# When the quarter sums of a token operand are made: behind the fifth and the sixth tile's rows, or all behind the fifth's

## The chip, the cores and the metric

The kernel runs on one core of one Trainium2 chip. The metric is device time in microseconds (us), the median of several runs. TensorE (PE in the profile) multiplies matrices and PEld loads its weights; VectorE (DVE), ScalarE (ACT) and GpSimd (POOL) work element by element; SyncE (SP) issues DMAs. Each engine runs its own queue of instructions in order and waits on semaphores of the others.

## The reference, cut to what matters

Two layers of a bidirectional encoder trunk on 1024 tokens and 16 meta tokens of width 1024: a mixer (gated DeltaNet and a short convolution) and then a SwiGLU feed-forward of inner width 2816, each with an RMSNorm before it and a residual after it. Only the feed-forward's first matrix product matters here:

```python
def swiglu(h, w_gate_up, w_down):
    gate, up = jnp.split(h @ w_gate_up.astype(h.dtype), 2, axis=-1)
    return (jax.nn.silu(gate) * up) @ w_down.astype(h.dtype)
...
h = h + swiglu(rmsnorm(h, norm2_w[l]), w_gate_up[l], w_down[l])
```

Everything is float32. The kernel splits each operand in two parts (a rounded `hi`, copied by ACT, and a rest `lo = x - hi`, made by DVE) and makes each product with three matmuls.

## The kernel before, in words

A layer goes through input projection, the DeltaNet scan, output projection, gate-and-up product, down product. The stage of this change is gate and up: a loop over 22 tiles `f` of 128 inner channels, numbered from 0, so that the "fifth tile" is `f == 4` (`NE = 4`) and the "sixth" is `f == 5`.

For each tile the gate and the up weights are two 128-column strips of 1024 rows. The kernel takes gate and up, the two halves of the 1024 inputs and the two halves of the tokens as a 2 by 2 matrix product, and makes it with seven products in place of eight (a Strassen-Winograd scheme): `p1` to `p7`, with weight sums and differences (`S1` at L1464, `S2` at L1465, `S3` at L1486, `S4` at L1485) and token operands that are the same for all tiles, `T["B11"]`, `T["B21"]`, `T["T1"]` to `T["T4"]` and `T["B22"]`, made before the loop. Each weight operand is split by `w_op` (L1104 on ACT, L1105 on DVE) into one of seven slots, which come free as PE has read them. The weights come by DMA (L1456 to L1459) into small rings of buffers.

Tiles 6 to 17 are taken in pairs, even and odd. Their `p3`, the product of `S4` and `T["B22"]`, is not made alone: `block()` makes it for the two tiles together, again as a 2 by 2 product in seven smaller ones of a quarter of the tokens each (`bp`, matmuls at L1530 to L1532). For this it needs
- weights: `keep`, which is `S4` of the even tile (L1485), the odd tile's counterpart `s1t` (L1473), and `sm`, four sums and differences of the two (L1476 to L1479), all split by `w_op`;
- tokens: the four quarters of `T["B22"]` themselves and four sums of these quarters, split and kept in `TB[0]` to `TB[3]`. These are the quarter sums of this change. They are made once in a layer, by `block_operands`, and read by every pair.

The sums are made in scratch tiles `c4k("t")`, each cut in two halves `va` and `vb`. The tag "c" of `c4k` has two buffers in the whole kernel, and `keep` and `sm` come from the same two. Tokens are 1040 columns in layer 0 and 1024 in layer 1, so a sum of two half-quarters works on 128 x 520 or 128 x 512 elements.

`row_end` closes a tile: it scales gate and up (L1438, L1439), applies silu (L1440), multiplies (L1441, `row_done`), and stores the row (L1445). `row_before` is the `row_done` of the tile before. `after(a, b)` makes instruction `a` wait for `b`.

The order on each engine is set when the kernel is built, by a planner that runs through the program with a model of times. Each instruction's rank is its place in the program unless the code gives it another; of the instructions that can start by the model, the one of the first rank goes next, and a tile gets a buffer of its ring when the model has one free. At run time each engine keeps that order.

The function `block_operands(i)` is called twice in a layer: with 0 after tile 4's `row_end` and with 2 after tile 5's. Each call makes two sums; its first instruction waits for the row just ended, and the second call's second sum needs the first call's second sum (`less`). The first pair of tiles that reads the result is 6 and 7.

## Time and profile before

| | us |
|---|---|
| median of 3 runs | 2468.67 |
| lowest and highest run | 2467.69, 2473.94 |
| the profiled execution | 2466.03 |
| its span, first to last instruction | 2464.3 |
| PE busy in the span | 2438.2 (99%) |
| DVE busy | 1834.9 (74%) |
| ACT busy | 1081.9 (44%) |

All times inside the profile count from the start of the span. The tiles of interest lie at 688 to 730 us in layer 0 and at 1908 to 1948 us in layer 1. A busy PE is not PE at its full pace: matmuls overlap, and their length also grows when the granted clock falls, so the number of matmuls in a stretch is read beside the busy time.

In a row of the timeline stand the start, the busy time, the engine, the line, the operation, the tile written and those read (buffer numbers left out), the shape, and in brackets how long the engine had been idle and what released it. Tiles named `a`, `b`, `P` are slices of large buffers that many operands share, so the line tells more than the name. In a row of a window stand the stretch, its length, the busy time and count of PE, PEld, DVE, ACT and POOL, the granted TensorE clock as a share, the DMA share and GB/s.

### The profile page before, as it was taken

How to read it: one execution, taken by the hardware profiler on the slowest of the kernel's cores; microseconds unless marked ns; L12 is line 12 of the kernel's file. 1: busy time of each engine (PE TensorE's matmuls, PEld its weight loads, DVE VectorE, ACT ScalarE, POOL GpSimd, SP SyncE). 2: the span in 40 equal slices, each digit the busy share in tenths (PEclk: the TensorE clock that was granted, in tenths of full speed). 3: DMA queues.
4: the chain of work that ended last, by engine and by line, in shares of the span. 5: the costliest groups of instructions: out<-in, count | busy, mean ns of one | idle time of the engine just before them, and what ended most of it. 6: DMA issues, size and time to landing. Idle time of an engine off the chain costs nothing. (4 is left out here: it accounts for less than half of the span.)

```text
span 2464.3 us, 45203 instructions
## 1 busy us (share of the span) xinstructions
PE 2438.2 (99%) x17602; PEld 2256.7 (92%) x17602; DVE 1834.9 (74%) x3436; ACT 1081.9 (44%) x2028; POOL 66.3 (3%) x157
## 2 busy tenths in 40 slices
PE   9999999999999999999999999999999999999998
PEld 8999999999999999999999988998978788888887
DVE  6888346769888887977657984457797888778775
ACT  6654434536333333444445543345453333334544
POOL 0120000000000000000001100000000000000002
PEclk9999999999999999999999999999999999999999
DMA  4445345534222224674224453445332222337641
GB/s 134 160 156 185 118 134 158 182 101 134 100 78 104 84 86 137 223 243 143 92 81 155 155 179 111 152 144 194 121 124 98 82 94 99 119 130 251 198 136 69
DMA packets 201322, 335.27 MB, mean 136 GB/s; under 512 B 23404, under 2 KB 88356, under 8 KB 201108
## 3 DMA queue, kind: packets, MB, share of 16 engines
q1 hardware_dynamic: 172996, 293.83, 36.0%
q10 hardware_dynamic: 25936, 34.19, 4.3%
q0 software_dynamic: 2176, 4.36, 0.6%
q8 instruction: 138, 2.26, 0.4%
q14 instruction: 76, 0.62, 0.1%
HBM read 250.31 MB, written 81.99 MB: 135 GB/s over the span
## 5 line engine op out<-in xcount | busy, mean ns | idle before, releaser
L168 PE MATMUL pacc<-a,whi 128*128 128x346 f32 (+1 forms) x800 | 260.1, 326 | 0.7 <-ACT whi L138 0.4
L170 PE MATMUL pacc<-a,wlo 128*128 128x346 f32 (+1 forms) x800 | 259.0, 325 | 0.1
L168 PE MATMUL pacc<-b,whi 128*128 128x346 f32 (+2 forms) x672 | 232.4, 347 | 0.0
L170 PE MATMUL pacc<-b,wlo 128*128 128x346 f32 (+2 forms) x672 | 231.5, 346 | 0.0
L169 PE MATMUL pacc<-a,whi 128*128 128x346 f32 (+1 forms) x681 | 221.8, 326 | 0.2 <-DVE a L189 0.2
L138 ACT ACTIVATE whi<-raw 128x512 fp32r<-128x512 f32 x166 | 104.4, 631 | 236.8 <-PE pacc L169 195.1
L169 PE MATMUL pacc<-b,whi 128*128 128x346 f32 (+2 forms) x580 | 200.1, 345 | 0.0
L139 DVE TENSOR_TENSOR wlo<-raw,whi 128x512 fp32r<-128x512 f32 x166 | 114.0, 688 | 53.5 <-ACT whi L138 52.8
L168 PEld LDWEIGHTS pacc<-a,whi 128*128 128x128 f32 x800 | 150.5, 188 | 3.0 <-issue 1.0
L170 PEld LDWEIGHTS pacc<-a,wlo 128*128 128x128 f32 x800 | 150.7, 189 | 1.4 <-issue 0.8
L170 PEld LDWEIGHTS pacc<-b,wlo 128*128 128x128 f32 x672 | 126.4, 188 | 10.2 <-issue 1.7
L168 PEld LDWEIGHTS pacc<-b,whi 128*128 128x128 f32 x672 | 126.4, 188 | 9.8 <-issue 0.8
L169 PEld LDWEIGHTS pacc<-a,whi 128*128 128x128 f32 x681 | 128.3, 188 | 4.1 <-issue 2.1
L169 PEld LDWEIGHTS pacc<-b,whi 128*128 128x128 f32 x580 | 109.2, 188 | 7.9 <-issue 1.0
L1104 ACT ACTIVATE whi<-rw 128x512 fp32r<-128x512 f32 (+1 forms) x82 | 49.8, 615 | 107.4 <-PE pacc L1125 36.1
L1104 ACT ACTIVATE b<-rw 128x512 fp32r<-128x512 f32 (+1 forms) x63 | 38.7, 620 | 102.3 <-PE pacc L1125 29.0
L331 DVE TENSOR_TENSOR b<-pacc,rstd 128x346 f32<-128x346 f32 (+1 forms) x63 | 32.3, 513 | 49.0 <-PE pacc L170 46.3
L1104 ACT ACTIVATE a<-rw 128x512 fp32r<-128x512 f32 (+1 forms) x63 | 38.5, 618 | 64.4 <-PE pacc L1125 17.2
L331 DVE TENSOR_TENSOR a<-pacc,rstd 128x346 f32<-128x346 f32 (+2 forms) x59 | 32.6, 553 | 42.5 <-PE pacc L170 41.9
L1105 DVE TENSOR_TENSOR wlo<-rw,whi 128x512 fp32r<-128x512 f32 (+1 forms) x82 | 54.1, 666 | 9.9 <-ACT whi L1104 9.4
L1368 ACT ACTIVATE P<-a 128x512 fp32r<-128x512 f32 x63 | 38.3, 625 | 25.4 <-PE pb L1684 19.7
L1368 ACT ACTIVATE P<-b 128x520 fp32r<-128x520 f32 x63 | 37.2, 628 | 27.1 <-PE pacc L1684 20.1
(1129 smaller groups left out, 8019.0 us busy)
## 6 DMA issues: line engine op xcount, KB each, us to landing
raw<-in_w_in SPq DMA_DIRECT2D x110, 256.0 KB
raw<-in_w_gu SPq DMA_DIRECT2D x104, 256.0 KB
rw<-in_w_gu SPq DMA_DIRECT2D x88, 256.0 KB
rw<-in_w_dn SPq DMA_DIRECT2D x90, 192.0 KB
rec<-vkd SPq DMA_DIRECT2D x61, 256.0 KB
raw<-in_w_out SPq DMA_DIRECT2D x48, 256.0 KB
b<-ad SPq DMA_DIRECT2D x45, 260.0 KB
a<-ad SPq DMA_DIRECT2D x45, 256.0 KB
```

The source lines that it names most:

```text
L138: whi_done[0] = hasten(wpr, lambda: act(out=hi, in_=raw[:, 0:kk, :], func=AF.Copy))
L139: whi_done[1] = hasten(wpr, lambda: tt(out=lo, in0=raw[:, 0:kk, :], in1=hi.bitcast(F32), op=ALU.subtract))
L168: mm(ps[:, :n], wh, xh[:, n0:n1], start=(i == 0), stop=False)
L169: mm(ps[:, :n], wh, xl[:, n0:n1], start=False, stop=False)
L170: last_mm[0] = mm(ps[:, :n], wl, xh[:, n0:n1], start=False, stop=(i == K - 1))
L331: tt(out=t[:, n0:n1], in0=ps, in1=rstd[:, n0:n1], op=ALU.mult)
L1104: hasten(wpr, lambda: act(out=hi, in_=src, func=AF.Copy))
L1105: hasten(wpr, lambda: tt(out=lo, in0=src, in1=hi.bitcast(F32), op=ALU.subtract))
L1368: act(out=hi, in_=r, func=AF.Copy)
```

## The change

All four sums of a layer are now issued after tile 5's `row_end`, in two calls, and wait only for tile 4's row (`gate[0]`). The first call (`late` False) makes sums 0, 1 and 3 in one scratch tile, sum 3 in place over sum 1; the second (`late` True) makes sum 2 in another. In each call the difference `cx - cy`, which waits for no row, now stands first. Each sum is split right after it is made (`put`).

```diff
-        TB, us, rows, less = [], [], [], [None]
+        TB, us, rows, gate = {}, [], [], []
...
-        def block_operands(i):
+        def block_operands(late):
...
-            x, cx, y, cy, p, q = (b22, c22, b12, c12, b21, c21) if i else (b12, c12, b11, c11, b22, c22)
             va, vb = (t.rearrange("p (k e) -> p k e", k=2) for t in halves(c4k("t"), 2 * E))
-            after(tt(out=va, in0=x, in1=y, op=ALU.subtract), row_before)
-            tt(out=vb, in0=cx, in1=cy, op=ALU.subtract)
-            tt(out=va, in0=va, in1=vb, op=ALU.add)
-            tt(out=vb, in0=p, in1=less[0] if i else va, op=ALU.subtract)
-            tt(out=vb, in0=vb, in1=q, op=ALU.add)
-            less[0] = vb
-            for r, v in zip(rows[i:i + 2], (va, vb)):
-                h, w = (t.rearrange("p (k e) -> p k e", k=2) for t in halves(r, 2 * E))
+            x, cx, y, cy = (b22, c22, b12, c12) if late else (b12, c12, b11, c11)
+
+            def put(n, v):
+                h, w = (t.rearrange("p (k e) -> p k e", k=2) for t in halves(rows[n], 2 * E))
                 act(out=h, in_=v, func=AF.Copy)
                 tt(out=w, in0=v, in1=h.bitcast(F32), op=ALU.subtract)
-                TB.append((h, w))
+                TB[n] = h, w
+
+            tt(out=vb, in0=cx, in1=cy, op=ALU.subtract)
+            after(tt(out=va, in0=x, in1=y, op=ALU.subtract), gate[0])
+            tt(out=va, in0=va, in1=vb, op=ALU.add)
+            put(2 if late else 0, va)
+            for n, p, q, less in () if late else ((1, b22, c22, va), (3, b21, c21, vb)):
+                tt(out=vb, in0=p, in1=less, op=ALU.subtract)
+                tt(out=vb, in0=vb, in1=q, op=ALU.add)
+                put(n, vb)
...
-            if f in (NE, NE + 1):
-                block_operands(2 * (f - NE))
+            if f == NE:
+                gate.append(row_before)
+            if f == NE + 1:
+                block_operands(False)
+                block_operands(True)
```

## The prediction

> **What bounds the kernel now.** I read the page's busy table first, then the busy time and granted clock in 10 us windows over the whole span, then, where TensorE lost time, the waits of PE, the chain that ended last and the order of instructions on DVE.

> ```profile
> PE 2438.2 (99%) x17602; PEld 2256.7 (92%) x17602; DVE 1834.9 (74%) x3436; ACT 1081.9 (44%) x2028; POOL 66.3 (3%) x157
> 700.00:720.00 20.00, 20.00 (x169) 20.00 (x168) 17.31 (x32) 7.26 (x16) 0.00 (x0) 1.00 0.26 90
> 720.75:729.22 8.47, 6.55 (x38) 5.88 (x37) 7.11 (x14) 2.67 (x6) 0.00 (x0) 0.80 0.09 32
> 1900.00:1920.00 20.00, 20.00 (x88) 16.22 (x87) 15.94 (x24) 7.00 (x11) 0.00 (x0) 1.00 0.24 92
> 1935.35:1948.13 12.78, 7.06 (x29) 5.68 (x27) 12.39 (x23) 5.12 (x10) 0.00 (x0) 0.73 0.18 62
> ```

> TensorE sets the time: 99% of the span. A change that moves work on DVE and ACT can only matter where PE stops. The window rows read: stretch, its length, then busy time (count) of PE, PEld, DVE, ACT and POOL, and the granted clock. Ahead of the final tail only two of the 10 us windows have a clock under 1.00, and both are the first product block of a layer (tiles 6 and 7). Layer 0: 38 matmuls took 8.47 us; at the pace beside it (20/169 = 0.118 us) they need 4.5, so 4.0 us are lost. Layer 1: between the edges stand 24 narrow matmuls of the block (0.118 us each, 2.8) and three wide ones (20/88 = 0.227, 0.7) in 12.78 us, so 9.3 are lost. Together 13.3 us, 0.54% of the span: that is the most this change can win. Of it 1.9 (8.47 - 6.55) and 5.7 (12.78 - 7.06) is standing still, the rest, 2.1 and 3.6, slower pace.

> PE's waits (line that waited, what it waited for, us in total, times, longest) and the chain in layer 1 say for whom it stood still:

> ```profile
> PE pf L1530 <- ACT b L1104: 3.2, 1, 3.2
> PE pf L1532 <- DVE b L1105: 1.8, 1, 1.8
> PE pacc L1532 <- DVE a L1105: 1.1, 1, 1.1
> PE pa L1530 <- DVE a L1509: 0.7, 1, 0.7
> ```
> ```profile
> 1936.39 0.68 DVE a L1431
> 1937.07 0.60 DVE t L1426
> 1937.67 0.60 DVE keep L1485
> ```

> Each wait of the block's lines (L1530 to L1532) occurs once in the run, so the later block tiles have none of this size. In layer 1 the chain runs through the very instructions the change moves: the sums (L1426, L1431), then `keep`, the weight difference of tile 6 (L1485); `sm` (L1476), which holds the block's other weights, comes after them. The order on DVE shows why these follow each other:

> ```profile
> 1907.18 1.23 DVE L1441 TENSOR_TENSOR b<-b,b3f 128x1024 f32<-128x1024 f32 x1
> 1910.72 0.69 DVE L1422 TENSOR_TENSOR t<-a 128x512 f32<-128x512 f32 x1
> 1920.28 0.68 DVE L1426 TENSOR_TENSOR t<-t,a 128x512 f32<-128x512 f32 x1
> 1921.48 0.69 DVE L1473 TENSOR_TENSOR rw<-raw,rw 128x512 f32<-128x512 f32 x1
> 1922.95 0.69 DVE L1431 TENSOR_TENSOR a<-t,a 128x512 fp32r<-128x512 f32 x1
> 1928.81 0.69 DVE L1582 TENSOR_TENSOR b<-pb,b 128x512 f32<-128x512 f32 x1 [5.17 <-PE pb L1126]
> 1931.28 1.22 DVE L1441 TENSOR_TENSOR b<-b,a3f 128x1024 f32<-128x1024 f32 x1
> 1933.35 0.68 DVE L1422 TENSOR_TENSOR t<-a 128x512 f32<-128x512 f32 x1
> 1937.59 0.69 DVE L1485 TENSOR_TENSOR keep<-raw,rw 128x512 f32<-128x512 f32 x1
> 1939.92 0.69 DVE L1431 TENSOR_TENSOR b<-t,b 128x512 fp32r<-128x512 f32 x1
> 1941.13 0.42 DVE L1476 TENSOR_TENSOR sm<-rw 128x256 f32<-128x256 f32 x1
> ```

> Row 5 (the second L1441) ends at 1932.5; only then may the second call begin (1933.35). Both calls' scratch, `keep` and `sm` share two buffers (tag "c" in the code). The first call's buffer is held for `less` until the second call reads it (L1425), so `keep` comes at 1937.59; the second call's is held until its last split (1939.92), and `sm` follows at 1941.13. PE had run out of other work at 1935.35.

> **The change part by part.**

> *Count.* Before: two calls with 5 sums and 2 splits on DVE each, 14 in a layer, and 4 copies on ACT. After: 10 and 4 on DVE, 3 and 1 on ACT. Nothing is added; no DMA, no matmul. Cost of the amount itself: zero.

> *The second call leaves row 5's end.* Six of its seven DVE instructions stood behind row 5 (its L1423 is ungated and ran earlier). At the 0.6 us by which successive ones start (1937.07 to 1937.67 in the chain) that is 3.6 us of DVE work in a layer that goes from behind row 5 to before it. What it frees is worth more than its length: `keep` and `sm` no longer wait for row 5. Gated on row 4, ending at 1907.18 + 1.23 = 1908.4, 12 DVE instructions remain to be done (14 less the two ungated first differences). At 0.6 us that is 7.2 us, so 1915.6 at best. At worst they go at the present first call's pace: seven from 1910.72 to 1923.64, 1.85 us each, 22.1 us, so 1932.8. I take 1921, nearer the best: tile 7's preparation, which now shares that stretch with them, ranks behind the sums in the new order, tile 5's own read-outs come only as PE delivers them, and DVE stands idle 5.17 us before 1928.81. From `keep`'s place to the first block split is 0.7 us on DVE and another on ACT; to `sm` it is 3.5 (1937.59 to 1941.13). `sm` also needs L1473, at 1921.48 now; if the 3.6 us push that to 1925, `sm` is ready around 1929, its splits around 1932, still before 1935.35. So layer 1's stall goes whole: 9.3.

> ```profile
> 698.93 0.69 DVE L1431 TENSOR_TENSOR b<-t,b 128x520 fp32r<-128x520 f32 x1
> 708.75 1.23 DVE L1441 TENSOR_TENSOR a<-a,b3f 128x1040 f32<-128x1040 f32 x1
> 715.19 0.68 DVE L1485 TENSOR_TENSOR keep<-raw,rw 128x512 f32<-128x512 f32 x1
> 722.14 0.69 DVE L1464 TENSOR_TENSOR rw<-rw,rw 128x512 f32<-128x512 f32 x1 [1.36 <-DMA rw<-in_w_gu]
> 722.75 0.69 DVE L1105 TENSOR_TENSOR a<-sm,a 128x512 fp32r<-128x512 f32 x1
> ```

> Layer 0 has the same order: row 5 to 710.0, `keep` at 715.19. The last thing late there is the split of `sm` (722.75), queued on DVE behind an addition of tile 8 that waited for its load. That load takes a buffer which tile 7's work frees, so it too starts sooner when `keep` and `sm` do. With the worst pace (first call 689.4 to 699.6, seven, so 12 take 17.5 us from 688) the sums end at 705.5 and `keep` comes some 9 us earlier than now, against a stall of 4. I take all 4.0; if the load did not move, the 4.0 stay.

> *What the added DVE load may cost in tile 5.*

> ```profile
> 688.00:710.00 22.00, 22.00 (x186) 22.00 (x185) 19.78 (x35) 7.54 (x14) 0.00 (x0) 1.00 0.24 78
> 1908.00:1932.00 24.00, 24.00 (x105) 19.50 (x104) 18.61 (x29) 6.67 (x11) 0.00 (x0) 1.00 0.15 55
> ```

> From row 4's to row 5's end DVE has 2.2 us free in layer 0 and 5.4 in layer 1. Adding 3.6 overfills layer 0 by 1.4 us; what spills is tile 7's preparation, which finds the 3.6 us vacated behind row 5. So it costs PE between 0 and 1.4; I take the middle, 0.7. In layer 1 it fits.

> *The in-place fourth sum.* It overwrites the second sum, so DVE must wait until ACT has copied it.

> ```profile
> 1922.22 0.62 ACT L1430 ACTIVATE a<-t 128x512 fp32r<-128x512 f32 x1
> 1931.40 0.42 ACT L1104 ACTIVATE b<-rw 128x256 fp32r<-128x256 f32 x1 [8.56 <-issue]
> ```

> The present second sum is done at 1920.96 and its copy at 1922.84: 1.9 us, in which DVE had other instructions. Between 0 (others stand there) and 8.56 us (ACT once stood that long at a weight copy; everything behind the sum on DVE, tile 5's read-outs included, would wait). Nearest is the 1.9, under the idle time of tile 5 in layer 1 and inside the 0.7 in layer 0: no further cost.

> *The slower pace.* After standing still in layer 0, PE started a matmul every 0.21 us (726.43 to 726.64) instead of every 0.12, until 729.03:

> ```profile
> 726.43 0.42 PE L1531 MATMUL pf<-b,a 128*128 128x260 f32 x1
> 726.64 0.42 PE L1532 MATMUL pf<-b,a 128*128 128x260 f32 x1
> ...
> 729.03 0.36 PE L1125 MATMUL pf<-P,whi 128*128 128x260 f32 x1
> ```

> It follows the stall in both layers and no other place, so I count it as part of the stall. [...]

> **Sum.** 9.3 + 4.0 - 0.7 = 12.6 us. The profiled execution took 2466.03 us, so 2453.4; it lies 2.6 under the median of the runs (2468.67), so the median comes to 2456.1.

> **The rivals.**

> (B) Layer 1 is freed only in part. At the worst pace above, `keep` comes at 1932.8, 4.8 us sooner than now; layer 1 then saves 4.8 of its 9.3, layer 0 its 4.0: 8.8 less, 2459.9. For it: DVE was full from 1910 to 1923. Against: the 5.17 us gap after that.

> (C) The change doesn't do what it says: the sums have the lowest rank among tile 5's work, and if the last split of the third sum is still put behind row 5, one of the two "c" buffers stays taken, `sm` stays late, and the time stays at 2468.7.

> ```profile
> L1423 DVE TENSOR_TENSOR t<-b x2: 692/692/693, 607.7 to 690.0; 128x520 f32<-128x520 f32 x2
> ```

> For it: of the two ungated differences of layer 0 the second stood at 690.0 only, among the gated ones. Against: the first ran at 607.7, 82 us ahead of them, so what nothing holds is moved early.

> (D) Slower: the in-place sum becomes the wait. If ACT stands for w us in front of the second sum's copy, DVE stands with it, 2w in two layers, plus the 1.4 overfill less 1.8 left in layer 1 (5.4 - 3.6), plus slow pace as now (2.1 + 3.6), against the 13.3 won: 2w - 8. It breaks even at w = 4 and is over 7.4 us slower from w = 7.7. With the 8.56 of the ACT row: +9.1, 2477.8. Against it: the copies of the sums waited 1.9 at most. [...]

> **How the numbers follow.** Forecast 0.52, B 0.16, C 0.18, D 0.14. 0.3% (7.4 us) is about what a measurement of this kernel tells from no change; the limits are 2461.3 and 2476.1. The forecast and three quarters of B are faster: 0.64. The rest of B and nearly all of C are the same: 0.20. D and a little of C are slower: 0.16. The range runs from 2453 (all 13.3 off the fastest run, 2467.69, and 1.4 for other gains) to 2470 (C); it leaves out D. The forecast's own range is 2453 to 2458.5, its upper end being the sum in which layer 0's slow pace stays.

> **What would show it.** Right: all the sums start between row 4's and row 5's end; `keep` before row 5's end in both layers; no PE wait over 0.5 us on L1530 or L1532; granted clock 1.00 through both places; DVE over 21 us busy in the 22 of layer 0's tile 5. Wrong: a wait of DVE on the ACT copy in front of the in-place sum of over 4 us, a wait of PE at L1122 to L1126 in tile 6 or 7 that is not there now, or sums behind row 5.

## The result, and the profile after

The changed kernel takes 2461.54 us (median of 6 runs, 2458.01 to 2462.64) against 2468.99 (6 runs, 2467.69 to 2473.94): a ratio of 0.9964, 95% interval 0.9951 to 0.9977, so 7.45 us less. A second series gave 2459.91 against 2467.89 (0.9970, 0.9958 to 0.9982), 7.98 less. The sign is the forecast one and the time lies in the range, but the forecast was 12.6 us less. The profiled execution of after took 2462.45 us with a span of 2460.7. One execution, of the kernel called the gate alone below, took 11524.8 us for a reason that no profile shows, and is left out of every number.

At the two places of the change the profile looks as forecast. Windows of after (stretch, length, busy time and count of PE, PEld, DVE, ACT, POOL, granted clock, DMA share, GB/s):

```profile
690.35:712.35 22.00, 22.00 (x186) 22.00 (x185) 21.47 (x41) 9.01 (x16) 0.00 (x0) 1.00 0.32 105
718.00:728.00 10.00, 10.00 (x86) 10.00 (x85) 8.68 (x17) 4.40 (x9) 0.00 (x0) 1.00 0.20 67
1910.96:1937.57 26.61, 26.61 (x119) 21.66 (x119) 24.16 (x40) 9.25 (x16) 0.00 (x0) 1.00 0.19 70
1935.00:1948.00 13.00, 11.99 (x66) 10.02 (x65) 13.00 (x23) 6.04 (x11) 0.00 (x0) 1.00 0.28 99
```

The clock is 1.00 through both blocks. In layer 0, 86 matmuls fit into 10 us in which before had 56:

```profile
718.00:728.00 10.00, 8.08 (x56) 7.41 (x55) 8.10 (x17) 3.57 (x7) 0.00 (x0) 0.89 0.17 54
```

The order on DVE in layer 1 (timeline of after; `keep` is now L1489, `sm` L1480, the row's product L1445):

```profile
1909.73 1.23 DVE L1445 TENSOR_TENSOR b<-b,b3f 128x1024 f32<-128x1024 f32 x1
1913.28 1.28 DVE L1430 TENSOR_TENSOR t<-a 128x512 f32<-128x512 f32 x2
1927.65 0.68 DVE L1489 TENSOR_TENSOR keep<-raw,rw 128x512 f32<-128x512 f32 x1
1929.63 0.69 DVE L1426 TENSOR_TENSOR b<-t,b 128x512 fp32r<-128x512 f32 x1 [0.70 <-ACT b L1425]
1932.68 0.41 DVE L1480 TENSOR_TENSOR sm<-rw 128x256 f32<-128x256 f32 x1
1936.35 1.22 DVE L1445 TENSOR_TENSOR b<-b,a3f 128x1024 f32<-128x1024 f32 x1
1937.49 0.42 DVE L1483 TENSOR_TENSOR sm<-keep,sm 128x256 f32<-128x256 f32 x1
1938.42 0.68 DVE L1105 TENSOR_TENSOR b<-sm,b 128x512 fp32r<-128x512 f32 x1
1940.23 0.68 DVE L1105 TENSOR_TENSOR wlo<-sm,whi 128x512 fp32r<-128x512 f32 x1
```

All the instructions of the sums that wait for row 4 (1913.28 to 1930.32) lie between row 4's and row 5's end, and `keep` comes before row 5's product. Of the four instructions of `sm` three come before it and the last (1937.49) behind it, and so do the two splits of `sm` (1938.42 and 1940.23); in layer 0 all of `sm` comes behind row 5 (715.54 for a row that ends at 715.15). What the prediction did not have stands elsewhere, in the waits of PE:

```profile
PE pa L1122 <- DVE a L1573: 2.2, 1, 2.2
PE pa L1122 <- ACT b L1104: 1.6, 1, 1.6
PE pf L1534 <- ACT sm L1542: 1.0, 1, 1.0
```

The wait at L1534, the first of the block's lines (L1530 before), lies in layer 1's block. The wait of 2.2 us is new and lies in layer 1's tiles 0 to 2, some 75 us ahead of the changed instructions of that layer. Before, the read-out of tile 0 (L1569) stood early on DVE; after, it (L1573) stands three instructions further back, and the first of the two read-outs has moved behind an addition that waits 1.88 us for weights from DMA, though PE's last matmul into `pb` had ended at 1827.79. Timeline of before, then of after:

```profile
1828.63 0.68 DVE L1566 TENSOR_TENSOR a<-pb,b 128x512 f32<-128x512 f32 x1
1830.55 0.69 DVE L1464 TENSOR_TENSOR rw<-rw,rw 128x512 f32<-128x512 f32 x1 [1.24 <-DMA rw<-in_w_gu]
1831.76 0.69 DVE L1569 TENSOR_TENSOR a<-pa,a 128x512 f32<-128x512 f32 x1
```

```profile
1830.71 0.69 DVE L1468 TENSOR_TENSOR rw<-rw,rw 128x512 f32<-128x512 f32 x1 [1.88 <-DMA rw<-in_w_gu]
1831.92 0.68 DVE L1570 TENSOR_TENSOR a<-pb,b 128x512 f32<-128x512 f32 x1
1834.33 0.68 DVE L1573 TENSOR_TENSOR a<-pa,a 128x512 f32<-128x512 f32 x1
```

To see where each kernel gains and loses, I take the start of the n-th matmul of its trace (all traces hold 17602) less that in before, and list how this difference grows in seven stretches, named by the times of before. Negative is a gain. One profiled execution stands behind each row. Mostly near the blocks (694 to about 1080 and 1920 to 2100 us) the order of the matmuls differs from kernel to kernel, so that the n-th is not always the same one.

| kernel | to 688 | 688-735 | 735-1810 | 1810-1840 | 1840-1908 | 1908-1960 | to the end |
|---|---|---|---|---|---|---|---|
| after | +2.4 | -4.2 | +1.6 | +2.7 | 0.0 | -7.7 | +1.6 |
| after, second series | +0.8 | -4.2 | +0.3 | +3.9 | 0.0 | -7.7 | +0.3 |
| gate alone | +0.3 | -4.2 | +0.4 | +2.5 | 0.0 | -8.5 | -0.3 |
| gate alone, second series | +7.1 | -4.2 | +0.7 | +3.9 | 0.0 | -8.5 | -0.7 |
| gate alone, layer 1 order | +1.1 | -4.2 | -0.6 | +0.2 | 0.0 | -8.4 | -0.2 |
| after, layer 1 order | +0.7 | -4.2 | +1.7 | +1.6 | 0.0 | -7.7 | +0.8 |
| after, fourth sum not in place | +2.7 | -4.2 | +0.7 | +4.0 | 0.0 | -8.7 | -0.2 |
| after, gate on row 5 | +0.9 | +3.2 | +0.9 | +2.4 | 0.0 | +2.7 | +0.9 |
| before, one scratch tile | +1.5 | -3.2 | +0.7 | -0.2 | 0.0 | -2.1 | +0.4 |
| gate alone, one scratch tile | +1.0 | -4.2 | +2.6 | -0.2 | 0.0 | -4.8 | -0.3 |
| after, `keep` behind row 5 | +0.8 | -4.1 | +0.5 | +2.9 | 0.0 | -5.8 | +0.7 |
| after, `keep` later still | +0.8 | -1.6 | +0.8 | +1.9 | 0.0 | -0.4 | +0.4 |

The first column has nothing of the change in it: two executions of the same kernel differ there by 6.8 us (gate alone), so a single execution tells little by its whole time. The two block columns repeat within 0.1. So the two blocks gave 11.9 us, and layer 1's start took 2.7 to 3.9 of it back. Taken on to 2060 us, where the order of these kernels is the same again, layer 1's block is still at -7.7 in both profiles of after, but at -9.0 and -9.1 in the two of the gate alone and at -9.2 with the fourth sum not in place.

### The profile page after: what moved, and what is told of

It is laid out like the page before. It is cut to its first block, busy times and chain, and to the rows that moved or that the text cites. A ratio compares the mean times of both kernels' runs of the same rounds, so it can differ in the third digit from the quotient of the medians.

```text
span 2460.7 us, 45205 instructions
## 1 busy us (share of the span) xinstructions
PE 2436.8 (99%) x17602; PEld 2255.1 (92%) x17602; DVE 1834.7 (75%) x3436; ACT 1082.1 (44%) x2028; POOL 66.4 (3%) x157
## 5 line engine op out<-in xcount | busy, mean ns | idle before, releaser
L1104 ACT ACTIVATE whi<-rw 128x512 fp32r<-128x512 f32 (+1 forms) x82 | 49.9, 616 | 107.2 <-PE pacc L1125 36.7
L1104 ACT ACTIVATE b<-rw 128x512 fp32r<-128x512 f32 (+1 forms) x63 | 38.8, 620 | 98.4 <-PE pacc L1125 32.3
L1104 ACT ACTIVATE a<-rw 128x512 fp32r<-128x512 f32 (+1 forms) x63 | 38.5, 618 | 68.3 <-PE pb L1125 17.5
L1105 DVE TENSOR_TENSOR wlo<-rw,whi 128x512 fp32r<-128x512 f32 (+1 forms) x82 | 54.1, 665 | 11.8 <-ACT whi L1104 11.1
```

Of the source, the lines that this page charges most:

```text
L1104: hasten(wpr, lambda: act(out=hi, in_=src, func=AF.Copy))
L1105: hasten(wpr, lambda: tt(out=lo, in0=src, in1=hi.bitcast(F32), op=ALU.subtract))
```

## The experiments

Theory 1: the gate does the work. What stalls the block is that `keep`, `sm` and their splits stand behind row 5 and the sums on DVE. Theory 2: PE waited for the sums themselves, or the new grouping and the in-place sum matter. Theory 3: the missing gain went at layer 1's start, by the order of instructions there. The ratios are to the kernel before in the same series, whose medians were 2469.35, 2468.44 and 2467.89 us.

**The gate alone.** Before, with only the second call's gate moved to row 4.

```diff
-            after(tt(out=va, in0=x, in1=y, op=ALU.subtract), row_before)
+            after(tt(out=va, in0=x, in1=y, op=ALU.subtract), gate[0])
...
+            if f == NE:
+                gate.append(row_before)
```

> The kernel before, with one edit: the second call's first sum waits for tile 4's row in place of tile 5's. The grouping of the sums, their scratch and the sum that isn't in place stay as before. Theory 1 (the late gate keeps both 'c' buffers taken, and keep and sm come late): the gate alone is the change; both stalls go, some 2461.5 us, within 2 of the changed kernel. Rival (the regrouping and the in-place sum matter too): less than half of the gain, over 2465.

Measured: 2458.66 us (5 runs), ratio 0.9958 (0.9946 to 0.9971). The gate alone carries the whole gain; it came out 2.9 us under the changed kernel, not within the 2 expected. Both blocks lose their stall, layer 1's by 8.5 (9.0 up to 2060 us).

**The changed kernel with the gate on row 5.** Same grouping and in-place sum; only the gate is late.

```diff
-            if f == NE:
-                gate.append(row_before)
             if f == NE + 1:
+                gate.append(row_before)
                 block_operands(False)
                 block_operands(True)
```

> The changed kernel, with one edit: all sums wait for tile 5's row. Theory 1: twelve instead of six DVE instructions of the sums now stand between row 5 and the last split, 0.6 us each, so keep and sm come up to 3.6 us later than in the kernel before: stalls as before or longer, 2469 to 2476. Rival (the regrouping is the gain, not the gate): 2461 to 2463.

Measured: 2477.22 us (5 runs), ratio 1.0033 (1.0020 to 1.0046): slower than before, and a little beyond the range expected. Both calls now stand behind row 5 and the stalls are longer than ever. PE's waits:

```profile
PE pf L1534 <- ACT b L1104: 6.1, 1, 6.1
PE pacc L1534 <- ACT a L1104: 2.8, 1, 2.8
```

The grouping of the calls, with its in-place sum, is no gain of its own; with the old gate it loses 8 us.

**The fourth sum not in place.** After, with the second and fourth sum divided over the calls as before.

```diff
-            for n, p, q, less in () if late else ((1, b22, c22, va), (3, b21, c21, vb)):
-                tt(out=vb, in0=p, in1=less, op=ALU.subtract)
-                tt(out=vb, in0=vb, in1=q, op=ALU.add)
-                put(n, vb)
+            n, p, q, less = (3, b21, c21, sums[0]) if late else (1, b22, c22, va)
+            tt(out=vb, in0=p, in1=less, op=ALU.subtract)
+            tt(out=vb, in0=vb, in1=q, op=ALU.add)
+            sums.append(vb)
+            put(n, vb)
```

> After, with the second and the fourth sum grouped as before (the fourth is made in the second call's own scratch from the kept second one, nothing is overwritten). If the about 3 us by which the gate alone beat the changed kernel come from the in-place sum, directly or through the DVE order that it brings with it (in this kernel the read-outs of tile 0 in layer 1 stand as early as with the gate alone): about 2458.7 us, no wait over 1 us at pa L1122. If they come from the order of the calls (difference cx - cy first, both calls after tile 5): about 2461.5.

Measured: 2458.95 us (0.9962, 0.9949 to 0.9974). The expectation was wrong on one point: the wait at L1122 stayed (2.1 us), since the read-outs stand just as far back as in the changed kernel. Its layer 1 block is 1.0 better (-8.7 for -7.7, and -9.2 for -7.7 up to 2060 us), and it has no wait at the block's L1534. By the medians it seemed 2.6 better than after, as the gate alone seemed 2.9 better; so both kernels were run again.

**After and the gate alone, once more, on one chip.**

> The changed kernel once more, beside the gate alone on the same chip. If the 2.9 us between the two medians (2461.54 and 2458.66) are the cost of grouping and in-place sum (by the traces 0.8 in layer 1's block and 1.2 from there to 2300 us): 2460 to 2462, and 2 us over the gate alone. If they were chance (the clock halved early in the changed kernel's profile, at 55.1 us, where nothing differs): the two within 1 us.

> The gate alone once more: 2457.5 to 2459.5 us if its first median was no chance. Its trace should again lose about 2.5 us between 1810 and 1840 us against before, as one PE wait at pa L1122 or as a halved clock.

Measured: 2459.91 us for after (6 runs, 2457.70 to 2462.80) and 2458.32 for the gate alone (5 runs, 2457.29 to 2464.29), 1.6 apart with intervals that overlap (0.9958 to 0.9982 and 0.9954 to 0.9979). So a good part of the 2.9 us was chance; what repeats in the traces is 0.8 us of layer 1's block up to 1960 us and 1.3 to 1.4 up to 2060, where the changed kernel waits 1.0 us at L1534 for a copy (L1542). On ACT this copy (1940.94) stood behind another (L1509, 1940.29) that had waited for the DMA that stores row 5. No more than that can be laid to the grouping and the in-place sum, and since it is gone when the fourth sum is not made in place, it goes with how the second and the fourth sum are divided over the calls. The gate alone's second trace lost 3.9 us at layer 1's start and not the 2.5 expected: the wait at L1122 (2.1 us) and then a halved clock for 3.4 us.

**The order at layer 1's start.** After, with tile 2's first weight addition and its `S3` made to wait for tile 0's two read-outs, which puts the read-outs first again on DVE.

```diff
+            s1_ins = tt(out=s1t, in0=A21, in1=A22, op=ALU.add)
+            if last and f == 2:
+                after(s1_ins, gfirst[0])
...
+            s3_ins = tt(out=A21, in0=A11, in1=A21, op=ALU.subtract)
+            if last and f == 2:
+                after(s3_ins, gfirst[1])
...
+                gfirst.append(tt(out=part(g, 1, j), in0=pin(p), in1=part(u, 0, j), op=ALU.add))
...
+                gfirst.append(tt(out=part(g, 1, j), in0=pin(p), in1=part(g, 1, j), op=ALU.add))
```

> The changed kernel, and in layer 1 two preparations of tile 2 on DVE must follow the two sums that read tile 0's banks pb and pa (the order of the kernel before). Theory 3 (2.2 us of the gain were given back there, where PE waits at 1835 us for the bank pa): 2.2 less than the changed kernel, some 2459.3, and no wait of PE there over 0.5. Rival (that wait only takes the place of another): no difference, 2461.5.

Measured: 2458.31 us (5 runs, 2458.01 to 2459.68). The wait of 2.2 us is gone. In its profile the stretch still loses 1.6, because there the clock was halved for 3.4 us from 1821.0 (0.72 over 1820 to 1826), after a wait of 1.5 us that before has too (1.4). The same two edges on the gate alone:

> The gate alone, and in layer 1 tile 2's first weight addition and its S3 wait for tile 0's two read-outs, as in the run of the changed kernel with that order. If the loss of 2.5 us at 1810 to 1840 comes from read-outs queued behind an addition that waits for its weights: 0 to 1.7 us lost there instead (1.7 if the wait of 1.5 us at 1820 halves the clock for 3.4 us), 2456 to 2458 us. If the order there doesn't matter: as the gate alone, 2458.7.

Measured: 2457.27 us (5 runs, 2453.85 to 2458.78), ratio 0.9954 (0.9941 to 0.9966), the lowest median here. In its profile the stretch 1810 to 1840 loses 0.2, and the read-outs stand ahead of the addition:

```profile
1826.62 0.69 DVE L1571 TENSOR_TENSOR a<-pb,b 128x512 f32<-128x512 f32 x1
1827.82 0.69 DVE L1574 TENSOR_TENSOR a<-pa,a 128x512 f32<-128x512 f32 x1
1828.42 0.68 DVE L1465 TENSOR_TENSOR rw<-rw,rw 128x512 f32<-128x512 f32 x1
```

So the loss at layer 1's start is that order, and the change brought it along: the wait of 2.1 or 2.2 us, and in some executions a step at half clock behind it. (The first profile of the gate alone is less plain: the clock was halved there from 1819.5 to 1822.9 (matmuls 0.43 us apart, 0.23 behind it), before the read-outs, PE came to them later, and waited only 0.56 us.) The median of this kernel is only 1.05 under the gate alone's in the same series and 2.6 under after's, and all three intervals overlap; the stretch in the traces is the firmer evidence.

**One scratch tile.** Before, with the gate left on row 5, but all sums of a layer in one scratch tile, so that a "c" buffer is free for `keep` before the sums end.

```diff
-            va, vb = (t.rearrange("p (k e) -> p k e", k=2) for t in halves(c4k("t"), 2 * E))
+            if not less[0]:
+                less[0] = [t.rearrange("p (k e) -> p k e", k=2) for t in halves(c4k("t"), 2 * E)]
+            va, vb = less[0]
...
-            tt(out=vb, in0=cx, in1=cy, op=ALU.subtract)
-            tt(out=va, in0=va, in1=vb, op=ALU.add)
-            tt(out=vb, in0=p, in1=less[0] if i else va, op=ALU.subtract)
+            tt(out=va, in0=va, in1=cx, op=ALU.add)
+            tt(out=va, in0=va, in1=cy, op=ALU.subtract)
+            tt(out=vb, in0=p, in1=vb if i else va, op=ALU.subtract)
```

> Before, with the gate of the second call left on row 5, but all sums of a layer made in one scratch tile, so that one of the two c buffers is free for keep early and keep no longer stands behind the sums; sm still follows the last split of the sums, behind row 5. If the lateness of keep makes the larger part of the stall: the wait of the block on ACT b L1104 (3.2 us, layer 1) goes, the clock of layer 1's block stays at 1.00, about 2462 to 2465 us. If sm, the last of the chain, sets it: waits on the splits of sm (L1105) of 3 to 5 us in its place and 2467 to 2470.

Measured: 2463.19 us (10 runs), ratio 0.9978 (0.9969 to 0.9987): 5.3 us less without touching the gate. The time is the one expected if `keep` were the larger part, but the trace shows it for layer 0 alone. Layer 0 gets 3.2 of its 4.2, layer 1 only 2.1 of 8.5, and its clock is halved for 3.4 us (narrow matmuls 0.21 us apart from 1940.53, 0.12 from 1944.12). In layer 1 `keep` is early, and `sm`, still behind the late sums, is what PE waits for:

```profile
1910.12 0.69 DVE L1486 TENSOR_TENSOR keep<-raw,rw 128x512 f32<-128x512 f32 x1
1930.46 1.22 DVE L1442 TENSOR_TENSOR b<-b,a3f 128x1024 f32<-128x1024 f32 x1
1938.33 0.42 DVE L1477 TENSOR_TENSOR sm<-rw 128x256 f32<-128x256 f32 x1
```

```profile
PE pb L1531 <- ACT b L1104: 4.9, 1, 4.9
```

The shared buffers are thus part of the mechanism: `keep` was late because of them. But in layer 1 a late `sm` is enough for a stall, with `keep` early.

**The gate and one scratch tile together.**

> The gate alone and one scratch tile together: keep is early and the sums stand before row 5. If the stalls are gone with the gate alone already, nothing is left for this to win: 2457 to 2460 us, like the gate alone (2458.7). If a part of the loss at the blocks was left (the 1.0 us at L1534 in the changed kernel's layer 1, waits of 0.6 elsewhere): 2455 to 2457.

Measured: 2459.34 us (5 runs), no better than the gate alone. The number is the one expected if little is left to win, but by two differences that cancel. Layer 1's start loses nothing here, but its block gains only 4.8: `sm` comes at 1932.96 behind row 5's product (1931.83), PE waits 2.1 us for a weight split on DVE (L1105) until 1938.0, as `sm`'s first one (1937.26) ends, and the clock is halved for 3.4 us from 1939.3.

**`keep` behind row 5, the sums early.** After, with `keep` of tile 6 waiting for row 5.

```diff
-                tt(out=s4, in0=A12, in1=s2t, op=ALU.subtract)
+                s4_ins = tt(out=s4, in0=A12, in1=s2t, op=ALU.subtract)
+                if f == NE + 2:
+                    after(s4_ins, row_before)
```

> The changed kernel, and keep of tile 6 must wait for tile 5's row, while the sums stay early. Theory 1 (the block waits for its weights, because keep and sm are late): the stalls come back in good part, PE waits at the block's lines for splits of keep and sm, 2465 to 2470. Rival, theory 2 (the block waited for the summed token operands themselves): they are early here, so no difference to the changed kernel, 2460 to 2463.

Measured: 2461.53 us (11 runs), ratio 0.9972 (0.9963 to 0.9981). This is the number of theory 2. Theory 1 fell in the form in which I had put it: `keep` stands behind row 5 in both layers and the stalls do not come back. Layer 1's block gains 5.8, for 7.7 in the changed kernel, layer 0's 4.1. With no sums in between, `keep` follows row 5 after two short instructions and `sm` follows `keep`:

```profile
1932.12 1.22 DVE L1445 TENSOR_TENSOR b<-b,a3f 128x1024 f32<-128x1024 f32 x1
1934.19 0.68 DVE L1489 TENSOR_TENSOR keep<-raw,rw 128x512 f32<-128x512 f32 x1
1934.79 0.42 DVE L1480 TENSOR_TENSOR sm<-rw 128x256 f32<-128x256 f32 x1
```

So either row 5 is not what matters, or it is the work between row 5 and the weights. The next run tells these apart.

**DVE work put back behind row 5.** The run before, with `keep` computed six times more (the same values), so that DVE work stands behind row 5 again while the sums stay early.

```diff
                 if f == NE + 2:
                     after(s4_ins, row_before)
+                    for _ in range(6):
+                        tt(out=s4, in0=A12, in1=s2t, op=ALU.subtract)
```

> After, where tile 6's keep waits for row 5 (as in the run before it of that kind) and is then computed six times more, 3.6 us of DVE work at 0.6 us each between row 5 and sm, in place of the sums that stood there before the change. The sums themselves stay early. If what counts is the time at which keep and sm come behind row 5 (before the change keep at 1937.59 and sm at 1941.13 in layer 1): the block stalls again by some 2 to 4 us in a layer, 2464 to 2470 us. If it is the sums that PE waited for, or DVE work behind row 5 is harmless: 2461 to 2463.

Measured: 2468.14 us (11 runs), ratio 0.9999 (0.9990 to 1.0008): the whole gain is gone, with the sums as early as in the changed kernel. Layer 1's block loses 5.4 against the run before (-0.4 for -5.8), layer 0's 2.5. On ACT the first copy of `keep` waits for the last of the repeats, and PE waits for that copy:

```profile
1943.53 0.63 ACT L1104 ACTIVATE b<-keep 128x512 fp32r<-128x512 f32 x1 [5.06 <-DVE keep L1493]
```

```profile
PE pf L1538 <- ACT b L1104: 6.6, 1, 6.6
```

Six instructions of 0.6 us are 3.6 us; other DVE work that stood ready was set between them (a row's scaling of 1.22 us among it), so the delay was nearer 7. Theory 2 falls: PE did not wait for the sums but for the weights behind them. The refined theory 1 stands: what stalls the block is the length of the DVE work between row 5's end and the splits of `keep` and `sm`, and the change shortens it. That `sm` alone can be late enough is shown by the one scratch tile; a late `keep` with an early `sm` cannot be had, as `sm` is made from `keep`.

## Why the prediction was right or wrong

*The bound and the two places*: right. The gain is made at the two blocks and nowhere else, and the moved gate makes it.

*Layer 0, 4.0*: right, -4.2 in nearly every kernel with the early gate.

*Layer 1, 9.3*: right in mechanism, mis-sized. It gave 7.7. The gate alone gave 8.5 up to 1960 us and 9.0 up to 2060, nearly the whole term, so 1.3 goes with the division of the sums over the calls, most of it the 1.0 us at L1534; 0.3 is left unexplained. That wait also goes against one of my signs, no PE wait over 0.5 us on L1530 or L1532: L1534 is the line that was L1530. My account was also too simple: waiting for row 5 is cheap (`keep` behind row 5 kept 5.8 of 7.7), a queue of sums behind row 5 is dear (with the gate on row 5 that block lost 2.7).

*The sums done at 1921, `sm` at 1929, its splits at 1932*: the estimate was too early. The sums ended at 1930.32 in a trace that runs 2.5 us behind before's at that point, so about 1927.8 in before's time, nearer my worst pace (1932.8). The splits of `sm` started at 1938.42 and 1940.23, 1935.9 and 1937.7 in before's time, later than the 1935.35 that I had set as the limit. I had counted on DVE's idle time; it was 24.16 us busy in the 26.61 between the rows, and row 5 itself ended 5.1 us later (1937.57 for 1932.5), 2.5 of it from that shift. PE did not stop for them all the same: `keep` was split sooner, and no wait for a split stands among those of the block. So the stall went with less in hand than my account had.

*DVE overfill in layer 0, 0.7*: nothing was lost. DVE was 21.47 busy in 22.00 and row 5's end moved from 709.98 to 715.15 us (2.4 of it the shift at the start of the trace), but PE did 186 matmuls in 22 us from row 4's end, as before.

*The in-place sum*: no cost of the kind I weighed. In layer 1 the longest DVE wait for a copy of the sums is the 0.70 before 1929.63, far from the 4 us at which rival D decides. But without the in-place sum layer 1's block is 1.5 us better up to 2060 us, so "no further cost" was wrong by about that; no run parts the overwriting from the other division of the sums that comes with it. The 8.56 us that I took as the upper price was no delay of ready work: ACT stood until PE's matmul of 1930.92 (L1125) had ended, at 1931.3 (in after the same copy, at 1933.99, shows a wait of 1.52 us for that line), and its next two instructions then waited 1.15 and 1.23 us more.

*The slower pace counted with the stall*: right. The halved clock of layer 0's block (725.77 to 729.18 before) was 0.50, and PE had been idle for 1.87 of the 3.41 us before it. With the waits gone it is 1.00 there in both profiles of after (718 to 728 us). No run shows the 2.1 us staying, on which the upper end of the forecast's own range, 2458.5, rests: layer 0's block gained 4.2.

*The sum, 12.6*: this is the step that failed. It had "count: zero" and no term for instructions outside the change. The planner orders the whole program, and with the change it set layer 1's tile 0 read-outs behind an addition that waits for DMA. That cost 2.7 and 3.9 us in the two profiles of after. 11.9 less 2.7 to 3.9 leaves 8.0 to 9.2; the medians fell by 7.45 and 7.98. The rest, up to 1.8, lies in stretches in which executions of one kernel differ by as much.

*The rivals*: B gave nearly the time (2459.9 forecast for it, 2461.5 and 2459.9 measured), by luck: its layer 1 saves 4.8, the measured one 7.7, and the rest was lost elsewhere. C and D did not occur. The list of what would show the forecast wrong named a new PE wait at L1122, but in tiles 6 and 7; it came at that line, in tiles 0 to 2.

What stays open: why the planner takes the other order there. It set the read-outs back in after, in after with the gate on row 5, with `keep` behind row 5 or with the fourth sum not in place, and in the gate alone; it did not with `keep` later still (whose +1.9 there is a halved clock at 1822.4, 0.94 over 1810 to 1840), nor in either kernel with one scratch tile. Neither the gate nor the grouping orders these cases.

## What to carry to other kernels

Where an engine is 74% busy, as DVE here, and another waits for it, look not for the instruction that waits but for how much ready work stands in its queue between the late event and what the waiting engine needs; moving that work ahead of the event won 5.8 us in layer 1's block here, even with the needed instruction itself still behind the event. Where an order is planned for the whole program, compare the traces from start to end after a local change: here a quarter to a third of the gain was given back 75 us ahead of the layer's changed code, and in the traces two explicit edges got it back. And compare stretch by stretch before trusting a difference of 3 us between medians of five or six runs.

## What the runs showed of the hardware

The pause of 1.2 to 1.9 us at L1122 near 1820 us, present in before and after alike, was followed by a halved clock in the profiles of the gate alone (first series), of after with layer 1's order and of after with `keep` later still, and not in the others. Where the steps fall does not explain all of this: after 1.64 us within one step the clock stayed at 1.00 (gate alone with layer 1's order), and after 1.54 us within one step it was halved (after with layer 1's order). What decides between 1.2 and 1.8 us stays open.

A step of 3.413 us at a clock of 0.50 costs about 1.7 us, an estimate from these two numbers. The second profile of after fits it: it lost 3.9 us at layer 1's start, by a wait of 2.2 us and one such step (clock 0.93 over 1815 to 1840). So, by the same estimate, a wait of 1.5 us in this kernel costs 1.5 or 3.2 us. This is part of why two executions of one program differ: of the 6.8 us between the two profiles of the gate alone ahead of 688 us, some 3.9 arose at three such steps in the second of them (at 9.4, 57.2 and 210.8 us).
